# Two up projections with the weights stationary, the first one's operand normed per token tile, modulation product in rows of 1024

## The chip, the core and the metric

The kernel runs on one core of a Trainium2 chip. TensorE (PE in the views) multiplies, VectorE (DVE) and ScalarE (ACT) do element-wise work, GpSimd (POOL) small odds and ends, and SyncE (SP) issues nearly all loads. The metric is device time in microseconds of one execution, the median of several.

## The reference, cut to what matters

Two transformer blocks on 256 tokens of width 2048, in float32, one after the other. Each ends in a feed-forward part with a causal convolution over three tokens:

```python
def conv_ffn(h, w_up, conv_w, conv_b, w_down):      # w_up 2048 x 11264, w_down 5632 x 2048
    up = h @ w_up
    up_p = jnp.pad(up, ((0, 0), (CONV_WIDTH - 1, 0), (0, 0)))
    c = conv_b + sum(conv_w[j] * up_p[:, j:j + S] for j in range(CONV_WIDTH))
    gate, val = jnp.split(c, 2, axis=-1)
    return (jax.nn.silu(gate) * val) @ w_down
...
x = x + conv_ffn(rmsnorm(x, ffn_norm_g), w_up, conv_w, conv_b, w_down)     # first block
...
mod = (silu(c) @ w_mod + b_mod)                     # second block: 2048 -> 6 * 2048, one row
h = rmsnorm_2(x, ffn_pre_w) * (1 + sc_f) + sh_f
x = x + g_f * rmsnorm_2(conv_ffn_2(h, w_up, ffn_conv_w, w_down), ffn_post_w)
```

In front of the feed-forward parts stand the input projections, attention and pooling of the first block, the gated linear attention and short convolution of the second, and an output projection (`w_out`, 2048 x 2048) in each.

## The kernel before, in words

**Products.** Each float32 operand is split in two parts, `hi` (rounded to float32r) and `lo` (what is left); a product is hi*hi + lo*hi + hi*lo. `stream` (line 178 on) runs one pass: it takes 512 (or fewer) columns of a weight matrix, 128 rows at a time (a block `kb`), in loads of four blocks (1 MB, tile `raw`, three buffers). ACT copies two blocks to `hi` (L224), DVE subtracts to `lo` (L225), both with three buffers and placed some way ahead of their turn (`AHEAD`). The activations stand as the stationary operand, 128 features by 128 tokens, the weights move, 512 columns. With two token tiles that is six matmuls per block (L189 hi, L190 lo, L191 the activations' own lo part), 96 in a pass over 2048 rows; the output has tokens on the partitions. `lead` and `trail` put off the second token tile's matmuls at the start or end of a pass, so that the first tile's operand can be used, or the first tile's sums can be worked on, while the second catches up.

**The up passes.** `feed_forward` (L619 on) runs 22 passes over `w_up` (11 pairs of gate and value), each 512 columns wide: ACT copies the two sums to `ev` (L630 or L632), TensorE transposes them to features on the partitions (L270, eight transposes of 128 x 128 into four `aux` banks), ACT and DVE convolve from there (L640 or L643, two at L645 per 128 features), and of the value part DVE and ACT make the `act` operand (L650 to L652) for the down passes. Then four passes over `w_down`, 44 blocks each.

**Between w_out and the first up pass.** `add_residual` (L593) adds each 512-column chunk to `X`, ACT takes the sums of squares, and `operand_chunk` transposes the chunk (eight transposes, L270 `aux<-ident,X`) and splits it, chunk by chunk while the next chunk's pass runs. The norm's factor per token is applied later, when ACT copies the up sums (L632, `scale`).

**Background.** The product silu(c) @ w_mod is cut in 96 jobs, a list that `stream` draws from: each group of four blocks adds a rate (`MOD_IN`, `MOD_UP`, ...) to a counter, and a full counter takes one job. A job loads 1 MB of `w_mod` (tile `rawm`, out of the same three `raw` buffers) and adds four rows of 512 to `macc` on DVE (L306); every fourth job four transposes (L319) and a sum turn `macc` by features.

**Order.** A scheduler places the instructions on each engine; what stands in the program earlier has the better rank, `high_priority` moves it up. PSUM has eight banks: four for `mm`, four for `aux`. All tiles called `big`, `op`, `act`, `gc`, `hl` share sixteen buffers.

## Time and profile before

| | |
|---|---|
| median of 3 runs | 2304.84 us (2304.08 to 2308.02) |
| the profiled execution, its own time | 2303.8 us |
| its span | 2302.0 us |
| TensorE busy | 2264.5 us, 98% |
| VectorE busy | 1575.2 us, 68% |
| ScalarE busy | 1162.9 us, 51% |
| GpSimd busy | 28.6 us, 1% |
| read from memory | 512 MB, 224 GB/s |

Read first which engine is busy nearly all the time, then the chain of work that ended last, then the stretches by stage, and in a stretch how far apart the starts of two instructions of that engine stand: a matmul's own duration in these views includes filling and draining and overlaps the next one's, so that costs are read from starts, not from durations.

### The profile page before, as it was taken

How to read it: one execution, taken by the hardware profiler on the slowest of the kernel's cores; microseconds unless marked ns; L12 is line 12 of the kernel's file. 1: busy time of each engine (PE TensorE's matmuls, PEld its weight loads, DVE VectorE, ACT ScalarE, POOL GpSimd, SP SyncE). 2: the span in 40 equal slices, each digit the busy share in tenths (PEclk: the TensorE clock that was granted, in tenths of full speed). 3: DMA queues.
4: the chain of work that ended last, by engine and by line, in shares of the span. 5: the costliest groups of instructions: out<-in, count | busy, mean ns of one | idle time of the engine just before them, and what ended most of it. 6: DMA issues, size and time to landing. Idle time of an engine off the chain costs nothing.

```text
span 2302.0 us, 27211 instructions
## 1 busy us (share of the span) xinstructions
PE 2264.5 (98%) x10541; PEld 1875.0 (81%) x10541; DVE 1575.2 (68%) x2093; ACT 1162.9 (51%) x1584; POOL 28.6 (1%) x46
## 2 busy tenths in 40 slices
PE   8999999999999999999999999999999999999998
PEld 8878888888888888888797888878888888888886
DVE  5775676778787878666656777776667676674444
ACT  5464554555555555444546444465555555554443
POOL 1001000000000000000000000000000000000000
PEclk9999999999999999999999999999999999999999
DMA  6657456677777777777567656764665666566554
GB/s 227 221 207 255 164 197 227 219 256 252 259 254 257 246 262 264 270 274 257 192 224 242 207 180 240 265 220 165 219 221 200 222 219 223 198 223 213 194 190 146
DMA packets 262391, 516.33 MB, mean 224 GB/s; under 512 B 8567, under 2 KB 21733, under 8 KB 261749
## 3 DMA queue, kind: packets, MB, share of 16 engines
q1 hardware_dynamic: 260256, 510.44, 64.3%
q0 software_dynamic: 1168, 3.77, 0.5%
q8 instruction: 82, 1.34, 0.2%
q10 hardware_dynamic: 837, 0.37, 0.1%
q14 instruction: 48, 0.39, 0.0%
HBM read 512.44 MB, written 2.11 MB: 224 GB/s over the span
## 4 chain that ended last, share of the span: by engine, by line
PE 83%; DVE 6%; DMA 5%; issue 4%; ACT 2%; POOL 0%; SPq 0%; DVEq 0%; POOLq 0%; ACTq 0%
PE mm L190 26%; PE mm L191 26%; PE mm L189 26%; DMA rawm<-in_w_mod 3%; PE aux L270 3%; DVE lo L225 2%; DVE macc L306 1%; ACT hi L224 1%; DMA raw<-in_w_in 1%; PE aux L831 1%; DMA raw<-in_w_down 0%; PE aux L319 0%; DMA raw<-in_w_up 0%; PE aux L578 0%; PE aux L568 0%
## 5 line engine op out<-in xcount | busy, mean ns | idle before, releaser
L225 DVE TENSOR_TENSOR lo<-raw,hi 128x1024 fp32r<-128x1024 f32 (+3 forms) x763 | 914.7, 1202 | 562.3 <-ACT hi L224 560.3
L224 ACT ACTIVATE hi<-raw 128x1024 fp32r<-128x1024 f32 (+3 forms) x763 | 794.3, 1044 | 950.5 <-PE mm L191 768.8
L189 PE MATMUL mm<-hi,op 128*128 128x512 f32 (+3 forms) x2380 | 923.4, 388 | 4.6 <-ACT op L723 2.1
L190 PE MATMUL mm<-lo,op 128*128 128x512 f32 (+3 forms) x2380 | 921.7, 387 | 6.1 <-DVE lo L225 6.1
L191 PE MATMUL mm<-hi,op 128*128 128x512 f32 (+3 forms) x2380 | 919.5, 386 | 0.2 <-DVE op L724 0.2
L189 PEld LDWEIGHTS mm<-hi,op 128*128 128x128 f32 x2380 | 447.8, 188 | 92.4 <-ACT op L723 3.2
L190 PEld LDWEIGHTS mm<-lo,op 128*128 128x128 f32 x2380 | 447.9, 188 | 91.5 <-DVE lo L225 9.3
L191 PEld LDWEIGHTS mm<-hi,op 128*128 128x128 f32 x2380 | 447.7, 188 | 85.6 <-DVE op L724 2.0
L306 DVE SCALAR_TENSOR_TENSOR macc<-rawm,cact,macc 128x512 f32<-128x512 f32 x360 | 269.4, 748 | 43.6 <-DMA rawm<-in_w_mod 37.6
L190 PE MATMUL mm<-lo,act 128*128 128x512 f32 x672 | 262.1, 390 | 0.3 <-DVE lo L225 0.3
L189 PE MATMUL mm<-hi,act 128*128 128x512 f32 x672 | 262.1, 390 | 0.0
L191 PE MATMUL mm<-hi,act 128*128 128x512 f32 x672 | 261.8, 390 | 0.0
L645 DVE SCALAR_TENSOR_TENSOR gc<-aux,cw,gc 128x255 f32<-128x255 f32 (+1 forms) x352 | 147.8, 474 | 7.1 <-ACT gc L643 6.5
L190 PEld LDWEIGHTS mm<-lo,act 128*128 128x128 f32 x672 | 126.2, 188 | 27.6 <-DVE lo L225 1.4
L189 PEld LDWEIGHTS mm<-hi,act 128*128 128x128 f32 x672 | 126.2, 188 | 26.2
L191 PEld LDWEIGHTS mm<-hi,act 128*128 128x128 f32 x672 | 126.2, 188 | 25.9
L270 PE MATMUL aux<-ident,ev 128*128 128x128 f32 x352 | 55.3, 280 | 0.3
L270 PEld LDWEIGHTS aux<-ident,ev 128*128 128x128 f32 x352 | 37.1, 140 | 19.2 <-ACT ev L630 9.9
L640 ACT ACTIVATE gc<-aux,cb,cw 128x256 f32<-128x256 f32 x88 | 42.6, 564 | 3.4 <-PE aux L270 3.4
L651 ACT ACTIVATE act<-gc 128x512 fp32r<-128x512 f32 x44 | 27.7, 629 | 26.0 <-DVE gc L650 26.0
L630 ACT ACTIVATE ev<-mm 128x512 f32<-128x512 f32 x44 | 26.1, 594 | 27.1 <-PE mm L191 26.0
L632 ACT ACTIVATE ev<-mm,rs 128x512 f32<-128x512 f32 x44 | 30.0, 686 | 19.4 <-PE mm L191 19.4
(214 smaller groups left out, 993.3 us busy)
## 6 DMA issues: line engine op xcount, KB each, us to landing
raw<-in_w_up SPq DMA_DIRECT2D x176, 1024.0 KB, 4.9
rawm<-in_w_mod SPq DMA_DIRECT2D x96, 1024.0 KB, 5.4
raw<-in_w_down SPq DMA_DIRECT2D x88, 1024.0 KB, 5.1
raw<-in_w_in SPq DMA_DIRECT2D x72, 1024.0 KB, 5.2
raw<-in_w_out SPq DMA_DIRECT2D x32, 1024.0 KB, 6.1
raw<-in_w_in SPq DMA_DIRECT2D x12, 736.0 KB, 4.8
raw<-in_w_in SPq DMA_DIRECT2D x8, 704.0 KB, 5.4
raw<-in_w_in SPq DMA_DIRECT2D x4, 672.0 KB, 4.1
```

Source lines behind the costliest of these rows:

```text
L189: nc.tensor.matmul(ps[t][:, :n], a[:, tt], hi, start=st, stop=False)
L190: nc.tensor.matmul(ps[t][:, :n], a[:, tt], lo, start=False, stop=False)
L191: nc.tensor.matmul(ps[t][:, :n], b[:, tt], hi, start=False, stop=sp)
L224: nc.scalar.activation(hi[:, :, :n], r, AF.Copy)
L225: nc.vector.tensor_sub(lo[:, :, :n], r, hf[:, :, :n])
L270: nc.tensor.transpose(ps[:width, t * P:(t + 1) * P], src_of_t(t), ident)
L306: nc.vector.scalar_tensor_tensor(acc, raw[:, b], cact[:, k:k + 1], acc, op0=ALU.mult, op1=ALU.add)
L630: nc.scalar.activation(ev[t], ps, AF.Copy)
L632: nc.scalar.activation(ev[t], ps, AF.Identity, scale=evac_scale[:, t:t + 1])
L640: nc.scalar.activation(cv, ps[:, :S], AF.Identity, bias=cb[:, fb:fb + 1], scale=cw[2][:, fb:fb + 1])
L645: nc.vector.scalar_tensor_tensor(cv[:, back:], ps[:, :S - back], cw[2 - back][:, fb:fb + 1], cv[:, back:], op0=ALU.mult, op1=ALU.add)
L651: nc.scalar.activation(act[j][:, two, 0, :], gc[:, 1, two], AF.Copy)
```

## The change

- All up passes but the first of each feed-forward part go through a new function, `stream_up`. The weight tile is the stationary operand, 128 rows by 128 features, and the activations move: `hi` of the weights against both parts of the activations side by side (512 columns: 256 tokens of hi, 256 of lo), then `lo` of the weights against the hi part (256 columns), into the first half of the same bank. The output has features on the partitions, in four banks, which are taken by turns from `aux` and from `mm`. To finish, ACT copies the second half of a bank, DVE adds the first, and the convolution reads the sum from there: there are no transposes and no `ev` copies of 512.
- The first up pass of each part stays as it was, with `lead=16`.
- The operand of the first feed-forward part is made by `Modulated`, which the second one uses already: per token tile, after all four chunks, norm (`finish`), then transposes, scale and split (`split`). The last pass over `w_out` has `trail=14`, and no background jobs.
- The background product takes rows of 1024: 12 pieces of eight jobs in place of 24 of four, each job two rows of 1024 for four of 512, and eight transposes at the end of a piece. The rates are moved a little.
- Some small tiles move into `scr`.

```diff
-MOD_IN, MOD_OUT, MOD_UP, MOD_DOWN = 0.22, 0.35, 0.4, 0.45
+MOD_IN, MOD_OUT, MOD_UP, MOD_DOWN = 0.24, 0.35, 0.36, 0.47
...
+    def stream_up(W, n0, tiles, evac, every):
+        flip[0] ^= 1
+        if flip[0]:
+            ps = [aux([P, 512]) for _ in range(4)]
+        else:
+            ps = [psm.tile([P, 512], F32, tag="mm", name=nm("mm")) for _ in range(4)]
+        for i0 in range(0, 16, 4):
+            raw = wp.tile([P, 4, 512], F32, tag="raw", name=nm("raw"))
...
+            for h in range(0, 4, 2):
+                hi, lo = split_pair(raw, h, 512)
+                for j in range(2):
+                    kb = i0 + h + j
+                    x = tiles[kb // 4][:, kb % 4]
+                    for f in range(4):
+                        fs = slice(f * P, (f + 1) * P)
+                        nc.tensor.matmul(ps[f], hi[:, j, fs], x.rearrange("p a b -> p (a b)"),
+                                         start=kb == 0, stop=False)
+                        nc.tensor.matmul(ps[f][:, :S], lo[:, j, fs], x[:, 0, :], start=False, stop=kb == 15)
...
+        for f in range(4):
+            evac(f, ps[f])
...
-                    holder["acc"] = sm.tile([P, 512], F32, tag="macc", name=nm("macc"), bufs=1)
+                    holder["acc"] = sm.tile([P, 1024], F32, tag="macc", name=nm("macc"), bufs=1)
...
-                for b in range(4):
-                    k = 4 * i + b
+                for b in range(2):
+                    k = 2 * i + b
...
-        operand_chunk(c, xt, g)
+            if c == 3:
+                mod1.finish(t)
...
+            stream(w_out, 512 * c, 512, K16, of(yt), add_residual(c), every=MOD_OUT if c < 3 else 0,
+                   trail=14 if c == 3 else 0)
+    xt = mod1.tiles
...
+                elif stationary:
+                    def up_evac(f, ps, part=part, col=col, gc=gc, j=j):
+                        u = small([P, 512], "ev", 3)[:, :S]
+                        nc.scalar.activation(u, ps[:, S:], AF.Copy)
+                        nc.vector.tensor_tensor(u, ps[:, :S], u, op=ALU.add)
+                        convolve(j, part, f, col // P + f, gc, act[j], u)
+
+                    stream_up(W, col, xt, up_evac, every if j else 0)
...
-    feed_forward(xt, A["w_up"], cw, cb, rs, A["w_down"], first_down, MOD_UP, MOD_DOWN)
+    feed_forward(xt, A["w_up"], cw, cb, None, A["w_down"], first_down, MOD_UP, MOD_DOWN, True)
```

TensorE between two up passes of the first part, before (`mm` are the sums, `ev` the copies that are transposed into `aux`):

```order
L191 MATMUL mm_722_3872<-hi_742_3999,op_486_2580 128x512
L189 MATMUL mm_751_4050<-hi_754_4054,op_483_2577 128x512
L270 MATMUL aux_745_4023<-ident_76,ev_719_3869 128x128
L270 MATMUL aux_746_4029<-ident_76,ev_719_3869 128x128
L270 MATMUL aux_747_4035<-ident_76,ev_719_3869 128x128
L270 MATMUL aux_748_4041<-ident_76,ev_719_3869 128x128
L190 MATMUL mm_751_4050<-lo_755_4055,op_483_2577 128x512
```

TensorE at such a place in the change, where a background piece ends (L280 and L282 are the two matmuls of `stream_up`, L361 the background's transposes):

```order
L280 MATMUL aux_675_3715<-op_554_3005,hi_698_3882 128x512
L282 MATMUL aux_675_3715<-op_554_3005,lo_699_3883 128x256
L280 MATMUL aux_676_3716<-op_554_3005,hi_698_3882 128x512
L282 MATMUL aux_676_3716<-op_554_3005,lo_699_3883 128x256
L361 MATMUL aux_693_3847<-ident_76,macc_418_2213 128x128 x4
L361 MATMUL aux_694_3853<-ident_76,macc_418_2213 128x128 x4
L280 MATMUL mm_706_3934<-op_551_3002,hi_711_3940 128x512
L282 MATMUL mm_706_3934<-op_551_3002,lo_712_3941 128x256
```

The eight transposes of the sums are gone from between the passes. The background's transposes stand between an `aux` pass and an `mm` pass here, and write two of the four `aux` banks that the pass before has just filled.

TensorE from the last pass over `w_out` into the first up pass, before (`ident_76,X_75` are the transposes of a chunk of `X`):

```order
L191 MATMUL mm_551_2953<-hi_573_3087,op_441_2347 128x512
L189 MATMUL mm_600_3163<-hi_603_3167,op_483_2577 128x512
L190 MATMUL mm_600_3163<-lo_604_3168,op_483_2577 128x512
L270 MATMUL aux_577_3109<-ident_76,X_75 128x128
L270 MATMUL aux_578_3114<-ident_76,X_75 128x128
L270 MATMUL aux_579_3119<-ident_76,X_75 128x128
L270 MATMUL aux_580_3124<-ident_76,X_75 128x128
L191 MATMUL mm_600_3163<-hi_603_3167,op_483_2577 128x512
```

The same place in the change (L668 are the transposes of the normed operand, tile `xs`; `hl` are the put-off weights):

```order
L191 MATMUL mm_532_2858<-hl_545_2937,op_440_2332 128x512
L668 MATMUL aux_555_3006<-ident_76,xs_550_2955 128x128 x4
L668 MATMUL aux_557_3018<-ident_76,xs_550_2955 128x128 x4
L668 MATMUL aux_559_3030<-ident_76,xs_550_2955 128x128 x4
L668 MATMUL aux_561_3042<-ident_76,xs_550_2955 128x128 x4
L785 MATMUL aux_569_3070<-ident_76,vstage_568_3068 128x88
L785 MATMUL aux_572_3076<-ident_76,vstage_571_3074 128x88
L189 MATMUL mm_584_3096<-hi_587_3100,op_551_3002 128x512
```

Before, four groups of eight transposes of `X` stood among the matmuls of four passes; now sixteen stand ahead of the first up matmul, and sixteen more some 19 matmuls later.

VectorE behind the end of a value pass of the first part, before (L645 is the convolution, L650 and L652 make `act`, L225 is the weights' `lo`; `aux` are the transposed sums):

```order
L225 TENSOR_TENSOR lo_918_5009<-raw_916_5006,hi_917_5008 128x1024
L645 SCALAR_TENSOR_TENSOR gc_842_4594<-aux_901_4936,cw1_589_3145,gc_842_4594 128x255
L645 SCALAR_TENSOR_TENSOR gc_842_4594<-aux_902_4942,cw1_589_3145,gc_842_4594 128x255
L645 SCALAR_TENSOR_TENSOR gc_842_4594<-aux_901_4936,cw0_586_3139,gc_842_4594 128x254
L645 SCALAR_TENSOR_TENSOR gc_842_4594<-aux_902_4942,cw0_586_3139,gc_842_4594 128x254
L645 SCALAR_TENSOR_TENSOR gc_842_4594<-aux_903_4951,cw1_589_3145,gc_842_4594 128x255
L650 TENSOR_TENSOR gc_842_4594<-gc_842_4594 128x512
L225 TENSOR_TENSOR lo_920_5025<-raw_916_5006,hi_919_5024 128x1024
```

The same place in the change (L752 adds the two halves of a bank, L721 is the convolution, L256 the weights' `lo`, L346 the background; `aux` are the sums of the pass that has ended):

```order
L256 TENSOR_TENSOR lo_776_4375<-raw_772_4352,hi_775_4374 128x1024
L752 TENSOR_TENSOR ev_762_4316<-aux_737_4140,ev_762_4316 128x256
L752 TENSOR_TENSOR ev_763_4322<-aux_738_4141,ev_763_4322 128x256
L752 TENSOR_TENSOR ev_764_4331<-aux_739_4142,ev_764_4331 128x256
L346 SCALAR_TENSOR_TENSOR macc_715_3980<-rawm_782_4436,cact_90,macc_715_3980 128x1024
L721 SCALAR_TENSOR_TENSOR gc_705_3933<-ev_762_4316,cw1_573_3078,gc_705_3933 128x255
L721 SCALAR_TENSOR_TENSOR gc_705_3933<-ev_763_4322,cw1_573_3078,gc_705_3933 128x255
L721 SCALAR_TENSOR_TENSOR gc_705_3933<-ev_762_4316,cw0_570_3072,gc_705_3933 128x254
L721 SCALAR_TENSOR_TENSOR gc_705_3933<-ev_763_4322,cw0_570_3072,gc_705_3933 128x254
L256 TENSOR_TENSOR lo_779_4397<-raw_777_4394,hi_778_4396 128x1024
L725 TENSOR_TENSOR gc_705_3933<-gc_705_3933 128x512
L721 SCALAR_TENSOR_TENSOR gc_705_3933<-ev_764_4331,cw1_573_3078,gc_705_3933 128x255
```

Before, three `lo` of the new pass stood ahead of the sums' work, and six instructions between the third and the fourth; now two stand ahead, and between the second and the third there are three additions, a background row of 1024 and four steps of the convolution.

## Rows read from the trace of the kernel before

**Rows 1.** The page: busy time by engine; chain that ended last; one group.

```profile
PE 2264.5 (98%) x10541; PEld 1875.0 (81%) x10541; DVE 1575.2 (68%) x2093; ACT 1162.9 (51%) x1584; POOL 28.6 (1%) x46
...
PE 83%; DVE 6%; DMA 5%; issue 4%; ACT 2%; POOL 0%; SPq 0%; DVEq 0%; POOLq 0%; ACTq 0%
...
L190 PEld LDWEIGHTS mm<-lo,op 128*128 128x128 f32 x2380 | 447.9, 188 | 91.5 <-DVE lo L225 9.3
```

**Rows 2.** Stretches: up passes 2 to 22 (both parts); an operand made by Modulated.

```profile
core 0: us, PE busy (x) PEld busy (x) DVE busy (x) ACT busy (x) POOL busy (x), PEclk, DMA share, GB/s
402.70:886.71 484.01, 483.11 (x2217) 396.14 (x2216) 384.13 (x521) 266.75 (x327) 0.00 (x0) 1.00 0.72 252
1130.28:1161.66 31.38, 28.35 (x129) 22.38 (x128) 20.94 (x36) 20.27 (x36) 2.92 (x6) 0.95 0.44 152
1570.71:2051.41 480.70, 480.43 (x2195) 393.97 (x2194) 332.32 (x437) 255.46 (x325) 0.00 (x0) 1.00 0.62 210
```

**Rows 3.** Timeline of PE: start, duration, instruction; three boundaries of up passes.

```profile
655.69 0.66 PE L270 MATMUL aux<-ident,ev 128*128 128x128 f32 x4
...
678.49 0.66 PE L270 MATMUL aux<-ident,ev 128*128 128x128 f32 x4
...
701.77 0.66 PE L270 MATMUL aux<-ident,ev 128*128 128x128 f32 x4
```

**Rows 4.** Timeline of PE: two widths, first and last of a run.

```profile
900.22 0.39 PE L190 MATMUL mm<-lo,act 128*128 128x512 f32 x1
...
909.28 0.39 PE L191 MATMUL mm<-hi,act 128*128 128x512 f32 x1
...
1188.64 0.32 PE L190 MATMUL mm<-lo,op 128*128 128x336 f32 x1
...
1198.00 0.32 PE L191 MATMUL mm<-hi,op 128*128 128x336 f32 x1
```

**Rows 5.** Timeline of PE: operand transposes of either kind, and what followed.

```profile
357.05 0.66 PE L270 MATMUL aux<-ident,X 128*128 128x128 f32 x4 [1.07 <-DVE X L593]
...
1130.28 1.91 PE L714 MATMUL aux<-ident,xs 128*128 128x128 f32 x16
1134.02 0.50 PE L189 MATMUL mm<-hi,op 128*128 128x512 f32 x1 [1.83 <-ACT op L723]
```

**Rows 6.** Groups by line and form, count, busy us, mean ns, idle before.

```profile
L225 DVE TENSOR_TENSOR lo<-raw,hi 128x1024 fp32r<-128x1024 f32 x153 | 186.3, 1221 | 69.8 <-ACT hi L224 69.3
...
L306 DVE SCALAR_TENSOR_TENSOR macc<-rawm,cact,macc 128x512 f32<-128x512 f32 x113 | 84.6, 749 | 10.3 <-DMA rawm<-in_w_mod 8.4
...
L645 DVE SCALAR_TENSOR_TENSOR gc<-aux,cw,gc 128x255 f32<-128x255 f32 x76 | 34.0, 474 | 0.0
...
L652 DVE TENSOR_TENSOR act<-gc,act 128x512 fp32r<-128x512 f32 x20 | 13.7, 684 | 0.2 <-ACT act L651 0.2
...
L640 ACT ACTIVATE gc<-aux,cb,cw 128x256 f32<-128x256 f32 x76 | 36.7, 564 | 2.5 <-PE aux L270 2.5
```

**Rows 7.** The same view of the whole span: 256 columns on DVE and ACT.

```profile
L865 DVE TENSOR_TENSOR E<-E,qk 128x256 f32<-128x256 f32 x14 | 5.8, 415 | 0.0
...
L630 ACT ACTIVATE ev<-mm 128x512 f32<-128x512 f32 x44 | 26.1, 594 | 27.1 <-PE mm L191 26.0
...
L570 ACT ACTIVATE big<-aux 128x256 f32<-128x256 f32 x8 | 2.9, 383 | 2.8 <-PE aux L568 2.8
```

**Rows 8.** Timeline of DVE in the first up passes: how closely instructions follow.

```profile
566.29 2.04 DVE L645 SCALAR_TENSOR_TENSOR gc<-aux,cw,gc 128x255 f32<-128x255 f32 x5
...
570.68 1.22 DVE L225 TENSOR_TENSOR lo<-raw,hi 128x1024 fp32r<-128x1024 f32 x1
...
572.41 1.22 DVE L225 TENSOR_TENSOR lo<-raw,hi 128x1024 fp32r<-128x1024 f32 x1
573.55 0.68 DVE L652 TENSOR_TENSOR act<-gc,act 128x512 fp32r<-128x512 f32 x1
...
603.64 3.11 DVE L306 SCALAR_TENSOR_TENSOR macc<-rawm,cact,macc 128x512 f32<-128x512 f32 x4
```

More of the change, by code (lines that the diff above doesn't have):

```diff
@@ L345, in body @@
     for i in (0, 1, 3, 2, 4, 5):
-        for c in range(4):
-            background.extend(mod_piece(4 * i + c, by_feature(i)))
+        for c in range(2):
+            background.extend(mod_piece(2 * i + c, by_feature(i)))
     ss = small([P, NT, 4], "ss")
@@ L602, in body @@
-    head, tail = list(range(8)), list(range(8, 16))
-    open_ps = []
-    for c in range(2):
-        open_ps.append(stream(w_out, 512 * c, 512, head, of(yt), None, last=False, every=MOD_OUT))
-        mix(c)
-    xt = pair_tiles(16)
-    for c in range(4):
-        if c < 2:
-            stream(w_out, 512 * c, 512, tail, of(yt), add_residual(c), ps=open_ps[c], first=False, every=MOD_OUT)
-        else:
-            stream(w_out, 512 * c, 512, K16, of(yt), add_residual(c), every=MOD_OUT)
-        operand_chunk(c, xt, g)
@@ L659, in conv_columns @@
-    def conv_columns(ap3, name):
-        tiles = []
-        for j in range(3):
-            tiles.append(wide_columns(ap3[j], f"{name}{j}"))
-        return tiles
-    def wide_columns(ap1, name):
-        stage = small([P, P], "vstage", 2)
-        nc.scalar.dma_start(stage[:88, :], ap1.rearrange("(r p) -> r p", p=P))
-        ps = aux([P, 512])
-        nc.tensor.transpose(ps[:, :88], stage[:88, :], ident[:88, :88])
-        dst = cst.tile([P, 88], F32, tag="wide_" + name[-1], name=nm(name))
-        nc.vector.tensor_copy(dst, ps[:, :88])
-        return dst
@@ L726, in body, with add_residual, go @@
     late = {}
+    mod1 = Modulated(vec("ffn_norm_g"))
+    def add_residual(c):
+        def go(t, ps):
+            cs = slice(c * 512, (c + 1) * 512)
+            nc.vector.tensor_tensor(X[:, t, cs], ps, X[:, t, cs], op=ALU.add)
+            mod1.chunk(t, c)
+            if c == 3:
+                mod1.finish(t)
+        return go
+    head, tail = list(range(8)), list(range(8, 16))
+    open_ps = []
+    for c in range(2):
+        open_ps.append(stream(w_out, 512 * c, 512, head, of(yt), None, last=False, every=MOD_OUT))
+        mix(c)
@@ new lines, in conv_columns, with wide_columns @@
+    def conv_columns(ap3, name):
+        tiles = []
+        for j in range(3):
+            tiles.append(wide_columns(ap3[j], f"{name}{j}"))
+        return tiles
+    def wide_columns(ap1, name):
+        stage = small([P, P], "vstage", 2)
+        nc.scalar.dma_start(stage[:88, :], ap1.rearrange("(r p) -> r p", p=P))
+        ps = aux([P, 512])
+        nc.tensor.transpose(ps[:, :88], stage[:88, :], ident[:88, :88])
+        dst = cst.tile([P, 88], F32, tag="wide_" + name[-1], name=nm(name))
+        nc.vector.tensor_copy(dst, ps[:, :88])
+        return dst
@@ L728, in first_down @@
+    cw = conv_columns(A["conv_w"], "cw")
+    cb = wide_columns(A["conv_b"], "cb")
     def first_down(c):
```

179 lines of the change are left out of this document (101 added, 78 removed).

## The prediction

> **What bounds the kernel now.** I read the page's busy times and chain first: TensorE is busy 98% of the span and 83% of the chain that ended last is its own work [rows 1]. Other engines matter only where TensorE waits for them. Then the stretches that the change touches. The 21 up passes from the second on take 484.01 us in the first part and 480.70 us in the second, with TensorE busy for all but a microsecond and its granted clock at 1.00, the upper level, 2.4 GHz, [rows 2]. So an up pass costs what TensorE has to do in it, and I price that from the starts of its instructions.
>
> Two such prices. From L190 at 900.22 to L191 at 909.28 are 40 matmuls of 512 columns: 226.5 ns each. From 1188.64 to 1198.00 are 61 of 336 columns: 153.4 ns each [rows 4]. The 176 columns between cost 73.1 ns, 0.4154 ns a column, and some 13.8 ns are left that do not depend on the width. A pass of 96 matmuls of 512 is 21.74 us. Passes begin 22.80 us apart (the transposes at 655.69 and 678.49), or 23.28 with four background transposes (678.49 to 701.77) [rows 3]. The eight transposes of the sums thus cost 1.06 us a pass, four of the background 0.48 us, and none of it is hidden.
>
> **The change, part by part.** The sum is made against the profiled execution's 2303.8 us; the median is 1.0 us above that.
>
> *Up passes.* Per block the six matmuls of 512 columns become four of 512 and four of 256: as many columns, two matmuls more. No row shows float32r on 256 columns. On the line of the two widths one costs 153.4 - 80 x 0.4154 = 120.2 ns. Bounds: below, 109 ns, the spacing of transposes, each of which loads its own 128 columns of weights for 128 columns of work ((1.91 - 0.27) us over 15) [rows 5]; above, the 153.4 ns of 336 columns. I take 120, since two widths lie on the line and only a limit of the load could bend it. A pass is then 64 x (226.5 + 120.2) ns = 22.19 us. Before: 964.71 us for 42 passes less 44 background transposes (by the counts: 2217 - 2016 - 168 = 33, and 11) at 0.48 us per four, 5.3 us, is 959.4 us. After: 42 x 22.19 = 932.0 us. **-27.4 us.** Transposes of the two passes that stay as they were are paid as before, those of the two last passes fall away, so the stretches' edges cancel.
>
> A rule of the Trainium skill gives another price: TensorE: Matmul & The Clock Gate, section Back-to-back issue gap, has a warm matmul cost its columns over 2.4 GHz plus 2.5 ns. By that the 1344 additional matmuls would cost 3.4 us in place of 18.5, and the time would be some 15 us lower; the rows of 512 and 336 columns show 13.8 ns, and I go by them.
>
> *Background.* 24 groups of four transposes become 12 of eight; four more in a row cost 4 x 109 ns: 12 x 0.92 - 24 x 0.48 = **-0.5 us**. Loads are as many and as large. On DVE the work shrinks (below).
>
> *Operand of the first part.* Before: four groups of eight transposes among passes that run on, 1.06 us each, and one wait of 1.07 us at 357.05 [rows 5]: 5.3 us. After, it is made as the second block's first operand is made, by the same function: from the first transposes at 1130.28 to the end of the next pass 31.38 us, 9.6 above a plain pass, with 1.83 us of waiting in one place and a mean clock of 0.95 in the stretch [rows 2, 5]. The put-off matmuls (`trail=14`, 42 of them, 9.5 us) cover the norm of the first token tile; what is late is the split of the first four blocks. **+4.3 us**; 0 if `trail=14` and `lead=16` cover more than the eight there, 9 if the clock falls for longer.
>
> *Banks after the first pass of part one.* The eight transposes fill all four `aux` banks, and the first `stream_up` pass wants the same four. TensorE waits for the copy of the second token tile (0.59, rows 7), then per bank for ACT's 0.56 and two steps of DVE; steps follow each other at (2.04 - 0.47)/4 = 0.39 us, eight of them take 3.1 us [rows 6, 8]. Of that about 5 us one matmul round (1.4 us) and the transposes run beside it: **+3 us**, between 0 and 5. Before, this was hidden, since the next pass had its own banks. In part two the first `stream_up` pass takes `mm` banks, and this does not arise.
>
> *Background transposes behind an `aux` pass.* Twice in part one they write banks whose sums were just finished: ACT's copy (0.38) and DVE's addition (0.42) come first [rows 7]. The first bank's last matmul is three pairs, 1.04 us, older than the pass's end: about 0.5 us each, **+1 us**, at most 2.5.
>
> *VectorE in part one.* Additions are new, 4 x about 0.34 a pass; background rows get cheaper: 4 x 0.787 ((3.11 - 0.75)/3) = 3.15 us a job becomes 2 x 1.32 (0.787 plus the 0.538 by which 1024 columns exceed 512, 1221 - 683 ns) = 2.65 us [rows 6, 8]. A pass has 8 x 1.14 (`lo`) + 8 x 0.39 + 1.36 + 1.2 (products, `act`) + 1.44 jobs x 2.65 = 18.6 us, of 22.2: 84%. Before it was 18.5 of 22.9. There is room on average, but behind a value pass three additions, a row of 1024 and four steps stand ahead of the third `lo`, and with what follows the fourth `lo` ends, counted from the pass's end, at 0.6 + 1.3 + 1.6 + 1.1 + 0.6 + 0.4 + 0.3 + 0.6 + 0.4 + 1.1 = 8.0 us, when TensorE wants it at 3 x 2.77 = 8.3 us. It is close: **+2 us** for part one, from 0 up to the second rival. Part two has half the jobs: nothing.
>
> Sum: -27.4 - 0.5 + 4.3 + 3 + 1 + 2 = -17.6, so 2286.2 us for the profiled execution and **2287 us** for the median.
>
> **The rivals.** *The weights' load shows (slower).* Before, each load had a matmul of 512 columns to hide behind; now every second one has 256, 107 ns of streaming. If the next load can begin only when the `lo` matmul begins, that matmul lasts as long as load and change-over. The spacing of transposes puts a load at 109 ns; with the 13.8 ns that is 123 ns, 2688 x 3 ns = 8 us, still faster (2295 us). It decides from 120.2 + 17.6 us/2688 = 126.7 ns; at the bound of 153.4 it is +89 us, 2376 us; halfway between, 137 ns, 2332 us. For it: no row has float32r under 336 columns. Against it: loads recorded as 188 ns [rows 1] follow each other at 153 ns without leaving the line [rows 4]. The Trainium skill (same page, section LDWEIGHTS) puts a load at its columns over 1.2 GHz, 107 ns for 128, which is a tie with the streaming and speaks against this change; the transposes' 109 ns agree.
>
> *VectorE becomes the bound in part one (no change).* If the tight place behind a pass's end costs 0.8 us in each of 21 passes, 17 us go back: 2304 us. For it: 84% busy, in order, with ACT's results to wait for (69.8 us of idle time ahead of `lo`, nearly all for ACT [rows 6]). Against it: before the change DVE had stretches as long without `lo` (566.29 to 570.68 [rows 8]), and TensorE was idle for under a microsecond of that part's 484 [rows 2].
>
> *The fixed part is smaller (faster).* If the `lo` matmul costs no more than the load's 109 ns, 2688 x 11 = 30 us more are gained: 2257 us.
>
> **How the numbers follow.** Forecast 0.70 (its own range 2275 to 2299: the bounds of the operand, bank and DVE terms, and 115 to 123 ns for the `lo` matmul); load shows beyond its point 0.10; DVE bound 0.13; smaller fixed part 0.07. The range from 2270 to 2307 adds the DVE rival and leaves out the load rival and most of the last. A measurement of this kernel can tell about 0.2%, 4.6 us, from no change. Faster by more: 0.70 + 0.07 + 0.02 of the DVE rival = 0.79; within: 0.10, nearly all DVE; slower: 0.10 from the load and 0.01 from DVE.
>
> **What would show it.** In the profile after: pairs of matmuls 346.7 ns apart in the up passes, the `lo` one's start 226.5 behind the `hi` one's and the next 120 later; 22.2 us from pass to pass, in both parts alike; no L270-like transposes of `ev` but in two passes; a wait of some 3 us at the start of part one's second pass for the `aux` banks; under 2 us of TensorE's idle time charged to `lo` in part one. The prediction is wrong if the pair takes more than 353 ns, if part one's passes come out over 23 us while part two's do not, or if the stretch from the last pass over w_out to the second up pass loses more than 15 us.

## The result, and the profile after

The changed kernel takes 2281.28 us (median of 4 runs, 2277.82 to 2282.99), the kernel before beside it 2304.46 us: a ratio of 0.9891, 95% interval 0.9875 to 0.9907, 23.2 us less where 17.6 were forecast. Its profiled execution took 2280.28 us, with a span of 2278.5 us. The rows that answer to [rows 1], from the page of the changed kernel, with the two matmuls of `stream_up` (L280 the one of 512 columns, L282 the one of 256) and the background's row:

```profile
PE 2248.5 (99%) x11549; PEld 1912.1 (84%) x11549; DVE 1601.4 (70%) x2071; ACT 1181.1 (52%) x1680; POOL 30.7 (1%) x47
...
PE 94%; DVE 2%; DMA 2%; ACT 1%; issue 1%; POOL 0%; SPq 0%; DVEq 0%; POOLq 0%; ACTq 0%
...
L280 PE MATMUL aux<-op,hi 128*128 128x512 f32 x1344 | 472.6, 397 | 1.8 <-ACT gc L717 1.8
...
L282 PE MATMUL mm<-op,lo 128*128 128x256 f32 x1344 | 375.5, 280 | 0.2 <-DVE lo L256 0.2
...
L346 DVE SCALAR_TENSOR_TENSOR macc<-rawm,cact,macc 128x1024 f32<-128x1024 f32 x180 | 230.5, 1281 | 22.7 <-DMA rawm<-in_w_mod 20.9
```

TensorE's share of the chain went from 83% to 94%, VectorE's from 6% to 2%, the loads' from 5% to 2%. So two things happened: TensorE's own work became less, and it waits less for others. The stretches (the last pass over w_out with the first up pass, up passes 2 to 22 of part one, the four down passes, the passes over w_out_2, up passes 2 to 22 of part two), columns as in [rows 2]:

```profile
348.89:402.33 53.44, 49.99 (x238) 40.49 (x236) 33.75 (x59) 32.15 (x57) 1.12 (x2) 1.00 0.50 178
402.33:879.17 476.84, 476.59 (x2720) 413.93 (x2721) 391.39 (x525) 266.48 (x362) 0.00 (x0) 1.00 0.70 247
879.17:1124.08 244.91, 243.07 (x1091) 201.48 (x1089) 161.43 (x161) 105.66 (x120) 0.54 (x1) 1.00 0.73 262
1432.60:1526.43 93.83, 92.61 (x428) 76.46 (x426) 72.56 (x92) 47.98 (x71) 2.04 (x2) 1.00 0.76 270
1555.94:2028.78 472.84, 472.82 (x2703) 411.78 (x2702) 355.01 (x488) 264.08 (x367) 0.00 (x0) 1.00 0.62 215
```

The two up stretches went from 484.01 and 480.70 [rows 2] to 476.84 and 472.84 us: 15.0 us, about half of the 27.4 forecast for them. The rest came from where the forecast had next to nothing: the passes over w_in are 3.9 us shorter, the first down passes 2.4, the passes over w_in_2 5.6.

**The pair of matmuls has two spacings.** TensorE's timeline at the start of two passes, columns as in [rows 3]:

```profile
493.79 0.40 PE L280 MATMUL aux<-op,hi 128*128 128x512 f32 x1
494.04 0.28 PE L282 MATMUL aux<-op,lo 128*128 128x256 f32 x1
494.15 0.40 PE L280 MATMUL aux<-op,hi 128*128 128x512 f32 x1
...
516.41 0.40 PE L280 MATMUL mm<-op,hi 128*128 128x512 f32 x1
...
653.33 0.40 PE L280 MATMUL mm<-op,hi 128*128 128x512 f32 x1
653.56 0.28 PE L282 MATMUL mm<-op,lo 128*128 128x256 f32 x1
653.68 0.39 PE L280 MATMUL mm<-op,hi 128*128 128x512 f32 x1
...
675.51 0.40 PE L280 MATMUL aux<-op,hi 128*128 128x512 f32 x1
```

From 493.79 to 516.41 are 64 pairs in 22.62 us (most passes of this kind take 22.61, 353.3 ns a pair); from 653.33 to 675.51 they take 22.18 us (22.187 unrounded, 346.7 ns a pair). I call the first spacing wide, the second narrow. The narrow sum is the forecast's 226.5 + 120.2 to the tenth; its halves are not. On average the short matmul starts 232 ns behind the long one and the next long one 115 ns behind that; in the wide pass it is 237 and 117 ns. Between the two spacings there is little: the passes of the trace keep one of the two for many passes and then change (at 617 to 625, 759, 1769, 1839 and 1904 us). 214 of the 336 groups of eight pairs stand at the wide spacing, some 27 of 42 passes, which costs 214 x 8 x 6.67 ns = 11.4 us against narrow spacing throughout. 27.4 less 11.4 is 16.0. The stretches are 15.0 us shorter, since the background's transposes (5.3 us before, 4.6 after) and 1.7 us of other delays stand in them too.

### The profile page after: what moved, and what is told of

It reads as the page before. It is cut to its first block, busy times and chain, and to the rows that moved or that the text cites. A ratio compares the mean times of both kernels' runs of the same rounds, so it can differ in the third digit from the quotient of the medians.

```text
span 2278.5 us, 29454 instructions
## 1 busy us (share of the span) xinstructions
PE 2248.5 (99%) x11549; PEld 1912.1 (84%) x11549; DVE 1601.4 (70%) x2071; ACT 1181.1 (52%) x1680; POOL 30.7 (1%) x47
## 4 chain that ended last, share of the span: by engine, by line
PE 94%; DVE 2%; DMA 2%; ACT 1%; issue 1%; POOL 0%; SPq 0%; DVEq 0%; POOLq 0%; ACTq 0%
PE mm L190 17%; PE mm L189 17%; PE mm L191 17%; PE aux L280 13%; PE mm L280 13%; PE aux L282 7%; PE mm L282 7%; DMA rawm<-in_w_mod 1%; PE aux L310 1%; DMA raw<-in_w_in 1%; PE aux L896 1%; PE aux L361 0%; DVE lo L225 0%; PE aux L910 0%; PE aux L621 0%
## 5 line engine op out<-in xcount | busy, mean ns | idle before, releaser
L225 DVE TENSOR_TENSOR lo<-raw,hi 128x1024 fp32r<-128x1024 f32 (+3 forms) x415 | 490.8, 1186 | 350.1 <-ACT hi L224 349.4
L224 ACT ACTIVATE hi<-raw 128x1024 fp32r<-128x1024 f32 (+3 forms) x415 | 426.9, 1031 | 560.0 <-PE mm L191 496.3
L256 DVE TENSOR_TENSOR lo<-raw,hi 128x1024 fp32r<-128x1024 f32 x336 | 409.3, 1221 | 192.3 <-ACT hi L255 191.4
L280 PE MATMUL aux<-op,hi 128*128 128x512 f32 x1344 | 472.6, 397 | 1.8 <-ACT gc L717 1.8
L280 PE MATMUL mm<-op,hi 128*128 128x512 f32 x1344 | 472.9, 397 | 0.0
L189 PE MATMUL mm<-hi,op 128*128 128x512 f32 (+3 forms) x988 | 378.9, 383 | 4.4 <-ACT op L303 2.3
L190 PE MATMUL mm<-lo,op 128*128 128x512 f32 (+3 forms) x988 | 375.7, 380 | 1.4 <-DVE lo L225 1.4
L191 PE MATMUL mm<-hi,op 128*128 128x512 f32 (+3 forms) x988 | 375.6, 380 | 0.5 <-DVE op L683 0.5
L282 PE MATMUL aux<-op,lo 128*128 128x256 f32 x1344 | 375.6, 280 | 0.1
L282 PE MATMUL mm<-op,lo 128*128 128x256 f32 x1344 | 375.5, 280 | 0.2 <-DVE lo L256 0.2
L280 PEld LDWEIGHTS aux<-op,hi 128*128 128x128 f32 x1344 | 252.1, 188 | 62.8 <-ACT gc L717 2.0
L280 PEld LDWEIGHTS mm<-op,hi 128*128 128x128 f32 x1344 | 252.2, 188 | 60.5
L282 PEld LDWEIGHTS aux<-op,lo 128*128 128x128 f32 x1344 | 253.4, 189 | 0.7 <-DVE lo L256 0.5
L282 PEld LDWEIGHTS mm<-op,lo 128*128 128x128 f32 x1344 | 253.2, 189 | 0.8 <-DVE lo L256 0.7
L346 DVE SCALAR_TENSOR_TENSOR macc<-rawm,cact,macc 128x1024 f32<-128x1024 f32 x180 | 230.5, 1281 | 22.7 <-DMA rawm<-in_w_mod 20.9
L189 PEld LDWEIGHTS mm<-hi,op 128*128 128x128 f32 x988 | 186.6, 189 | 38.6 <-ACT op L682 3.2
L191 PEld LDWEIGHTS mm<-hi,op 128*128 128x128 f32 x988 | 186.6, 189 | 33.4 <-DVE op L683 2.7
```

Source lines behind the costliest of these rows:

```text
L189: nc.tensor.matmul(ps[t][:, :n], a[:, tt], hi, start=st, stop=False)
L190: nc.tensor.matmul(ps[t][:, :n], a[:, tt], lo, start=False, stop=False)
L191: nc.tensor.matmul(ps[t][:, :n], b[:, tt], hi, start=False, stop=sp)
L224: nc.scalar.activation(hi[:, :, :n], r, AF.Copy)
L225: nc.vector.tensor_sub(lo[:, :, :n], r, hf[:, :, :n])
L256: nc.vector.tensor_sub(lo[:, :, :n], r, hi.bitcast(F32)[:, :, :n])
```

## The experiments

**Rows of 512 again.** The changed kernel with the old background product:

```diff
-                raw = wp.tile([P, 2, 1024], F32, tag="raw", name=nm("rawm"))
+                raw = wp.tile([P, 4, 512], F32, tag="raw", name=nm("rawm"))
...
-                for b in range(2):
+                for b in range(4):
```

> The changed kernel with the background product in rows of 512 again (24 groups of four jobs, four rows of 512 a job, four transposes a group); all else as changed. Theory A: the time gained outside the up passes (3.6 us in the passes over w_in, 2.5 in the first down passes, 5.6 in the passes over w_in_2) comes from the wider rows, which leave VectorE more room; then this kernel gives back some 12 us and the half microsecond of transposes, and runs in 2293 us, with the same pair spacings in the up passes. Rival B: those gains come from the background's jobs falling at other moments; then it gives back 2 us at most, 2281 to 2284 us.

2300.88 us, 0.9981 (0.997 to 0.9992) of the kernel before. So the wider rows are worth more in the changed kernel than even A said: some four fifths of its gain go with them. The stretches that answer to the third and fourth above:

```profile
883.72:1136.20 252.48, 246.41 (x1091) 200.70 (x1089) 169.01 (x196) 104.07 (x120) 0.54 (x1) 1.00 0.73 255
1449.55:1547.57 98.02, 94.87 (x429) 77.28 (x427) 74.99 (x105) 48.03 (x71) 2.10 (x2) 0.98 0.73 258
```

The down passes take 7.6 us more and the passes over w_out_2 4.2 us more, where the up form is the same; the passes over w_in_2 between them take 4.8 us more. VectorE has only 7.6 and 2.4 us more to do in the two stretches shown and is far from full; what is lost stands at single places (in the down passes 23 delays with 6.4 us together, in the changed kernel 0.2 us), the first of them just behind the up passes:

```profile
891.90 0.39 PE L189 MATMUL mm<-hi,act 128*128 128x512 f32 x1
893.64 0.50 PE L190 MATMUL mm<-lo,act 128*128 128x512 f32 x1 [1.35 <-DVE lo L225]
```

The two up stretches take 950.1 us here, as many as in the changed kernel, but not because nothing is lost there. Only 111 of the 336 groups were wide in this trace, which costs 5.9 us; transposes and delays make up 12.2 us of the 950.1, against 6.3 in the changed kernel. How many groups are wide differs from execution to execution, as a later run shows, and is worth up to 17.9 us, so it is also a part of what separates the medians in this section.

**Rows of 1024 alone.** The kernel before with that part of the change (rates and small tiles with it):

```diff
-                raw = wp.tile([P, 4, 512], F32, tag="raw", name=nm("rawm"))
+                raw = wp.tile([P, 2, 1024], F32, tag="raw", name=nm("rawm"))
```

> The kernel before with the background product in rows of 1024 (12 groups of eight jobs, the new rates, the small tiles in scr) and nothing else of the change. Theory A: the wider rows relieve VectorE wherever it runs close to TensorE, in either form of the up passes, so most of the 20 us that they were worth in the changed kernel show here too: the 12 us of the passes over w_in, the first down passes and the passes over w_in_2 at least, 2294 us or less. Theory B: they are worth 20 us only together with the stationary up passes, whose additions fill VectorE up; with the old up passes they give no more than the prediction's half microsecond of transposes and the small waits, 2302 to 2306 us.

2294.83 us beside 2305.71 us of the kernel before: 10.9 us less, 0.9945 (0.993 to 0.9961). A, though not all of the 20 us: the rest shows only together with the stationary form. Its profiled execution was the slowest of five and shows 5 us of the gain (2.7 in the passes over w_in); where the other 6 lie isn't shown.

**Everything but the stationary form.** The call of the second part gets the same `False`.

```diff
-    feed_forward(xt, A["w_up"], cw, cb, None, A["w_down"], first_down, MOD_UP, MOD_DOWN, True)
+    feed_forward(xt, A["w_up"], cw, cb, None, A["w_down"], first_down, MOD_UP, MOD_DOWN, False)
...
-                    stream(W, col, 512, K16, of(xt), evac, every=every)
+                    stream(W, col, 512, K16, of(xt), evac, every=every if j else 0,
+                           lead=0 if j or part else 16)
```

> The changed kernel with all up passes in the old form (activations stationary, eight transposes of the sums), both parts; the first part's operand normed per token tile and the rows of 1024 stay. By the prediction's working the up passes cost 959.4 us in the old form; in the changed kernel's trace they cost 932 us and 11.4 us of slow pairs, with a wait of 2 us for banks: this kernel should be 14 us above the changed one, 2295 us, if the stationary form brings what the pairs show, and 4 us above the kernel before with rows of 1024 alone, if the operand costs what the prediction said. If VectorE takes part of the stationary form's gain back, it is less than 14 us above the changed kernel.

2294.79 us, 0.9948 (0.9933 to 0.9963): 13.5 us above the changed kernel, as expected, and level with the rows of 1024 alone. The stretches that answer to the first, second and last above:

```profile
350.13:401.68 51.55, 50.37 (x233) 41.25 (x232) 32.65 (x55) 29.76 (x53) 1.12 (x2) 0.97 0.56 190
401.68:884.78 483.10, 482.81 (x2215) 396.24 (x2214) 365.85 (x448) 262.31 (x325) 0.00 (x0) 1.00 0.72 244
1562.48:2042.57 480.09, 479.82 (x2191) 393.63 (x2189) 326.94 (x406) 255.08 (x325) 0.00 (x0) 1.00 0.63 211
```

The up stretches, 963.19 us here and 949.68 in the changed kernel, differ by the same 13.5 us. The first stretch is 1.9 us longer in the changed kernel: the wait for the `aux` banks. In the run with rows alone it took 47.94 us, and the three passes ahead 2.0 us more than here: moving the operand costs 3.6 - 2.0 = 1.6 us by the traces and nothing by the medians.

**No background.** What sets the spacing? First the changed kernel without the product.

```diff
-        for c in range(2):
-            background.extend(mod_piece(2 * i + c, by_feature(i)))
+        pass
...
         nc.vector.tensor_copy(bmod, ps[:, :96])
+        nc.vector.tensor_copy(mod, bmod)
```

> The changed kernel without the background product: silu(c) @ w_mod is left out (its 96 loads, VectorE's rows and sums, TensorE's transposes), the modulation is the bias alone. In the changed kernel a pair of matmuls (512 and 256 columns) in an up pass takes either 346.7 or 353.3 ns, and stays with one of them over several passes. Theory P: which of the two is set where the row of matmuls was last broken, by a split part that comes late or by transposes, and then lasts; without background nothing breaks it, so each part keeps the spacing of its first stationary pass (353.3 in the changed kernel), 22.61 us a pass from the third to the last. Rival C: 353.3 is what other work on the memory (VectorE's rows, loads) costs; without background all pairs take 346.7 ns, 22.19 us a pass. Either way the time falls by the 11 us of transposes and by waits outside the up passes: about 2262 us by P, 2252 us by C.

The trace (2257.62 us) has the pairs of both parts at 346.7 ns, but for the first few. So the spacing stays where nothing comes between, as P has it, but not at the one that I took for given. The other three runs took 2267.56 to 2268.38 us; one part at the wide spacing would account for 21 x 0.43 = 9 of these 10 us, but they have no trace.

**Breaks without load.** The same, with eight transposes of a constant behind every fourth up pass:

```diff
                     stream_up(W, col, xt, up_evac, every if j else 0)
+                    if j and (2 * j + part) % 4 == (0 if cb is not None else 3):
+                        for _ in range(2):
+                            ps = aux([P, 512])
+                            for q in range(4):
+                                nc.tensor.transpose(ps[:, q * P:(q + 1) * P], ident, ident)
```

> The changed kernel without the background product (silu(c) @ w_mod is left out, the modulation is the bias alone), and with eight transposes of a constant on TensorE behind every fourth stationary up pass; no work for VectorE, no loads come with them. Without them all pairs of matmuls took 346.7 ns in the trace. Theory P (the spacing is set anew where the row of matmuls is broken, and lasts until the next break): the spacing changes, if it does, only at these places, and of the ten to twelve stretches between them some run at 353.3 ns, 22.61 us a pass. Rival C (353.3 ns is what VectorE's rows and the loads cost): all stretches run at 346.7 ns, 22.19 us a pass, and only the transposes' 0.92 us are added behind every fourth.

One pass of part one and one of part two:

```profile
450.16:472.78 22.62, 22.62 (x131) 19.60 (x130) 14.47 (x21) 12.86 (x18) 0.00 (x0) 1.00 0.58 186
1579.08:1601.26 22.18, 22.18 (x130) 19.56 (x129) 16.62 (x26) 12.71 (x19) 0.00 (x0) 1.00 0.60 190
```

All of part one ran wide, all of part two narrow; none of the ten groups of transposes changed it. Both theories lose something. C falls: wide spacing without any of VectorE's rows or the background's loads. And a break by transposes between passes is not enough, against P. What holds in these two runs is that a part enters with one of the two and keeps it.

**The changed kernel once more, as it is.**

> The changed kernel as it is, profiled once more. Theory P (which of the two spacings a part starts with, and where it changes, is decided anew in each execution): other passes run at 353.3 ns than in the first profile (28 of 42, beginning slow in both parts). Rival F (the program's order fixes it): the same passes, with changes at the same places.

2279.55 us, with 180 groups of 336 wide. Part one began wide, part two narrow, where it had begun wide in the first profile. In part two the spacing changed at the same three places in both, in opposite directions. The first of them, in the first profile (passes of 22.61 us before it, 22.19 behind it) and in this one (22.19, then 22.61):

```profile
1768.34 0.40 PE L280 MATMUL aux<-op,hi 128*128 128x512 f32 x1
1768.57 0.28 PE L282 MATMUL aux<-op,lo 128*128 128x256 f32 x1
1768.69 0.40 PE L280 MATMUL aux<-op,hi 128*128 128x512 f32 x1
```

```profile
1764.94 0.39 PE L280 MATMUL aux<-op,hi 128*128 128x512 f32 x1
1765.17 0.28 PE L282 MATMUL aux<-op,lo 128*128 128x256 f32 x1
1765.29 0.39 PE L280 MATMUL aux<-op,hi 128*128 128x512 f32 x1
1765.54 0.39 PE L282 MATMUL aux<-op,lo 128*128 128x256 f32 x1
```

The next `lo` was finished 0.26 and 0.06 us ahead of its first matmul here, and so at the third place; at the second stand the background's transposes, in the middle of a pass. In part one the places differ: the first profile has two changes there, this one eight, and of these ten nine stand at a `lo` that was finished less than 0.4 us ahead of its first matmul (the tenth at the background's transposes). Four others as late changed nothing in the first profile. So in the changed kernel a close `lo` or a row of transposes is where the spacing can change, not what it changes to. F falls.

**lo one block behind.** If a late `lo` changes the spacing, wanting it later should leave fewer changes:

```diff
-                        nc.tensor.matmul(ps[f][:, :S], lo[:, j, fs], x[:, 0, :], start=False, stop=kb == 15)
+                        if behind:
+                            lw, lx = behind
+                            nc.tensor.matmul(ps[f][:, :S], lw[:, fs], lx, start=False, stop=False)
+                    behind = lo[:, j], x[:, 0, :]
...
+        lw, lx = behind
+        for f in range(4):
+            nc.tensor.matmul(ps[f][:, :S], lw[:, f * P:(f + 1) * P], lx, start=False, stop=True)
```

So the first four long matmuls of a pass and its last four short ones stand in a row.

> The changed kernel with the matmuls of 256 columns one block behind: hi of a block by turns with lo of the block before, so that lo is wanted 1.4 us later and the alternation stays. Theory P: with lo never late the spacing of the pairs changes at the background's transposes and the starts of the parts alone, is 346.7 or 353.3 ns in between, and which it is decides between 2270 and 2288 us; the waits for lo go, about 2 us in part one. Rival L (353.3 ns comes from lo's lateness itself): all pairs at 346.7 ns, 2268 to 2270 us.

2290.55 us, 0.9929 (0.9914 to 0.9944), slower than the change and beyond P's 2288. In part two, where every `lo` was ready at least 2.2 us ahead of its matmul, all 21 passes ran wide. L falls: wide pairs with no late `lo`. In part one, where four were still less than 0.4 us ahead, the spacing changed seven times, five of them between two passes. Some 34 wide passes instead of 27 are 3 us of the 9; the last up pass took 24.9 us (22.2 in the changed kernel) and the down pass behind it 62.4 (60.8), another 4.

**Other orders in a block.** Four long and four short, eight and eight, and long, short, short, long:

```diff
-                    for f in range(4):
-                        fs = slice(f * P, (f + 1) * P)
-                        nc.tensor.matmul(ps[f], hi[:, j, fs], x.rearrange("p a b -> p (a b)"),
-                                         start=kb == 0, stop=False)
-                        nc.tensor.matmul(ps[f][:, :S], lo[:, j, fs], x[:, 0, :], start=False, stop=kb == 15)
+                    for f in range(4):
+                        nc.tensor.matmul(ps[f], hi[:, j, f * P:(f + 1) * P], x.rearrange("p a b -> p (a b)"),
+                                         start=kb == 0, stop=False)
+                    for f in range(4):
+                        nc.tensor.matmul(ps[f][:, :S], lo[:, j, f * P:(f + 1) * P], x[:, 0, :],
+                                         start=False, stop=kb == 15)
```

> The changed kernel with another order in a block: the four matmuls of 512 columns first, then the four of 256, in place of one of each by turns. Theory N: a matmul costs its columns and a fixed part, whatever stands beside it, and the 353.3 ns come only from the alternation: 4 x (226.5 + 120.2) = 1387 ns a block, 22.19 us a pass, and the time falls by the 11.4 us of slow pairs to 2270 us. Rival L: the load of the weights is what the 353.3 ns show, and behind a matmul of 256 columns a load of 256's matmul cannot hide: four matmuls of 256 in a row take 126.7 ns or more each, 1413 ns a block or more, 22.61 us a pass in all 42 passes, and the time rises to 2288 us or above.

Eight and eight:

```diff
+                for j in range(2):
+                    ...
+                        nc.tensor.matmul(ps[f], hi[:, j, f * P:(f + 1) * P], x.rearrange("p a b -> p (a b)"),
+                                         start=kb == 0, stop=False)
+                for j in range(2):
+                    ...
+                        nc.tensor.matmul(ps[f][:, :S], lo[:, j, f * P:(f + 1) * P], x[:, 0, :],
+                                         start=False, stop=kb == 15)
```

> As the run before, over two blocks: eight matmuls of 512 columns, then eight of 256, so that the lo part is wanted 1.6 us later than in the changed kernel. Theory N: 2 x 1387 ns for two blocks, 2270 us, and no matmul waits for lo. Rival L: 2 x 1413 ns or more, 2288 us or above. If the lateness of lo costs something by itself, this run is faster than the one before; if not, they are equal within 1 us.

Long, short, short, long:

```diff
+                        ...
+                        for go in (short, long) if f % 2 and 0 < kb < 15 else (long, short):
+                            go()
```

> The changed kernel with another order in a block: long, short, short, long (512, 256, 256, 512 columns) in place of long and short by turns, except in the first and the last block of a pass. By runs of four and of eight a pair took 350.8 and 349.2 ns, with one spacing throughout. Theory N (each switch between widths and each run adds a fixed part): runs of two lie between, one spacing of 346.7 to 351 ns, 22.2 to 22.45 us a pass, and the time is 2276 to 2288 us. If it comes out at 346.7 ns it beats the changed kernel by some 11 us, 2270 us. Rival P: two spacings as in the changed kernel, 2281 us.

| order | undisturbed pass | a pair | time | ratio to before |
|---|---|---|---|---|
| by turns (the change) | 22.19 or 22.61 us | 346.7 or 353.3 ns | 2281.28 us | 0.9891 (0.9875 to 0.9907) |
| four and four | 22.45 us | 350.8 ns | 2286.28 us | 0.9917 (0.9904 to 0.9931) |
| eight and eight | 22.35 us | 349.2 ns | 2281.02 us | 0.9892 (0.9879 to 0.9906) |
| long, short, short, long | 22.34 us | 349.1 ns | 2281.64 us | 0.9881 (0.986 to 0.9902) |

Each other order has one spacing, the same in every undisturbed pass, between the two. For the first two of them neither N's 346.7 nor L's 353.3 came; for the last N's range held (346.7 to 351 ns, 2276 to 2288 us), and P's two spacings did not come. None beats the change by more than the intervals. Eight and eight is 5.3 us faster than four and four; 4.3 of that are its pairs, so that the later `lo` brings no more than 1 us, which the noise hides.

The runs of four also show which of the two matmuls is dearer than the forecast's 226.5 and 120.2 ns:

```profile
700.01 1.09 PE L279 MATMUL aux<-op,hi 128*128 128x512 f32 x4
700.94 0.64 PE L282 MATMUL aux<-op,lo 128*128 128x256 f32 x4
701.42 1.09 PE L279 MATMUL mm<-op,hi 128*128 128x512 f32 x4
```

By the starts four long ones take 0.93 us, 232 ns each, and four short ones 0.48 us (118.6 ns each, unrounded over 12 us). With eight and eight it is 230 and 119 ns. In these orders it is the long one; why it is dearer here than in the down passes is open.

**The short matmul's size.** 128 columns in place of 256, and 320:

```diff
-nc.tensor.matmul(ps[f][:, :S], lo[:, j, fs], x[:, 0, :], start=False, stop=kb == 15)
+nc.tensor.matmul(ps[f][:, :P], lo[:, j, fs], x[:, 0, :P], start=False, stop=kb == 15)
```

> The changed kernel with the lo part of the weights multiplied by 128 columns in place of 256; the lo product of the second token tile is left out. Theory T (tie: the load of 128 columns of weights, 109 ns by the spacing of transposes, is as long as the streaming of 256 columns, and is what holds the short matmul up): the pair stays at 346 ns or falls by a few ns, and the time stays within 15 us of the changed kernel's 2281 us. Rival D (columns decide, the load is hidden): the short matmul falls by 128 x 0.4154 = 53 ns to 67 ns, the pair to 293 ns, and the time by some 140 us, to 2140 us, if ScalarE and VectorE keep up.

```diff
+nc.tensor.matmul(ps[f][:, :320], lo[:, j, fs], x.rearrange("p a b -> p (a b)")[:, :320],
+                 start=False, stop=kb == 15)
```

> The changed kernel with the lo part of the weights multiplied by 320 columns in place of 256 (the 256 of hi and the first 64 of lo, a product that the kernel leaves out otherwise). By the line of widths the short matmul takes 146.7 ns, the pair 373.3 ns, a pass 23.89 us. Theory T (the two spacings of the pair come from the tie of load and streaming): with 64 columns more the load is hidden with room, and all pairs in both parts have one spacing, 373 ns; 2281 - 11.4 + 71.6 = 2341 us. Rival D (the two spacings have another origin): again two, 373 and 380 ns, 23.89 and 24.32 us a pass, with stretches of either.

TensorE with 128 columns, then with 320:

```profile
700.13 0.22 PE L282 MATMUL mm<-op,lo 128*128 128x128 f32 x1
700.19 0.44 PE L280 MATMUL mm<-op,hi 128*128 128x512 f32 x1
700.47 0.22 PE L282 MATMUL mm<-op,lo 128*128 128x128 f32 x1
700.53 0.44 PE L280 MATMUL mm<-op,hi 128*128 128x512 f32 x1
```

```profile
700.01 0.40 PE L280 MATMUL aux<-op,hi 128*128 128x512 f32 x1
700.24 0.31 PE L282 MATMUL aux<-op,lo 128*128 128x320 f32 x1
700.39 0.40 PE L280 MATMUL aux<-op,hi 128*128 128x512 f32 x1
```

With 128 columns the undisturbed pair takes 340 ns (700.19 to 700.53; passes of 21.76 us): half the columns save 7 to 13 ns, not 53, and D falls. Less the 226.5 of a long matmul that is 113 ns, less the 232 of a long one in a row 108, close to the 109 of a transpose in a row [rows 5]. That it is the load which costs this is T's argument and not shown: the starts alone lie 60 ns behind the short one and 280 ns behind the long one. The Trainium skill (TensorE: Matmul & The Clock Gate, section LDWEIGHTS) puts a load at its columns over 1.2 GHz, an estimate of 107 ns for 128, and the rest of the pair agrees with it. With 320 columns the pair takes 380.0 ns in both parts, 24.32 us a pass, one spacing only, as T says; but not T's 373.3. By the starts the short one takes 146 ns, T's 146.7, and the long one ahead of it 234 in place of 226.5. Two spacings were seen only where a short matmul of 256 columns stands alone between long ones.

The time with 128 columns was 2344.08 us, 63 more, against T's 15. For the most part this is the waits' doing:

```profile
PE mm L282 <- DVE lo L256: 28.3, 23, 4.2
PE aux L282 <- DVE lo L256: 21.6, 20, 2.8
```

In the changed kernel these waits come to 0.2 us together. Another part is the clock, which fell at times. Here the engine had stood idle for 2.00 us before:

```profile
495.50 0.33 PE L282 MATMUL mm<-op,lo 128*128 128x128 f32 x1 [2.00 <-DVE lo L256]
...
497.16 0.74 PE L280 MATMUL mm<-op,hi 128*128 128x512 f32 x1
497.70 0.31 PE L282 MATMUL mm<-op,lo 128*128 128x128 f32 x1
497.80 0.73 PE L280 MATMUL mm<-op,hi 128*128 128x512 f32 x1
```

From 496.2 to 499.5 us the granted clock was 0.50, the lower level, 1.2 GHz, and a pair took 640 ns (497.16 to 497.80). Some 68 pairs of the up passes were as slow, which costs 20 us. The scheduler also gave VectorE another order here (in part one a row of the background stands just ahead of a `lo` 38 times, 26 times in the changed kernel), so this isn't the price of shorter passes alone; 2359.87 us with 320 columns is what its pairs make of it.

## Why the prediction came out

The bound was right, and so was the mechanism in the up passes: TensorE's own work sets their time, and it became less. That 2287 stood so near to 2281 is in part luck, two errors that cancel: the up passes gave 11.4 us less than forecast, the background 10.4 more.

| step | forecast | the runs |
|---|---|---|
| up passes | -27.4 us | -16.0: -27.4 at the narrow spacing, +11.4 for the wide one |
| background: transposes, rows | -0.5 | -10.9, by itself |
| operand of the first part | +4.3 | +1.6 by the traces, 0 by the medians |
| banks after the first pass | +3 | +1.9 |
| transposes behind an `aux` pass, VectorE in part one | +1, +2 | +1.7 together |
| sum | -17.6 | -21.7, measured -23.2 |

The 1.7 us are what the two up stretches (949.68 us) hold beside their pairs (932.0 + 11.4) and five groups of eight transposes (0.92 each). The -10.9 is the worth of the rows without the rest of the change; beside the stationary form it was 19.6 (2300.88 to 2281.28), so the table is one way of adding up, not the only one.

- **Up passes.** The step that failed is the price of a pair as the sum of two numbers, each read from rows of its own width in passes where the weights move. 226.5 + 120.2 ns is right for a third of the pairs; the others take 353.3. The runs of four and of eight put the excess on the long matmul (232 and 230 ns in place of 226.5); the short one took 119, no more than said. The rival "the weights' load shows" put its point at 126.7 ns for the short one, a pair of 353.2, so its price came in two thirds of the pairs, at the very point from which it eats the gain; and by the prediction's own sign (a pair over 353 ns) the forecast of this part was wrong there. Its reason, the load, is not shown, and the short matmuls in a row, each with a load of its own, speak against it. The other sign held: both parts behave alike.
- **Background.** This was the big miss. The prediction had found the cheaper rows (3.15 to 2.65 us a job; the means of 749 and 1281 ns make it 3.0 and 2.56) and used them only in part one's balance of VectorE. But jobs run beside nearly every stage, and one in front of a `lo` delays it. What TensorE waited for (time, times, longest), in the changed kernel with rows of 512:

```profile
PE mm L190 <- DVE lo L225: 5.1, 8, 1.3
...
PE aux L359 <- DVE macc L346: 3.1, 2, 2.7
```

and in the changed one, which has none of the second kind:

```profile
PE mm L190 <- DVE lo L225: 1.4, 2, 1.2
```

The same line for the kernel before and for the rows of 1024 alone:

```profile
PE mm L190 <- DVE lo L225: 6.4, 10, 1.2
```

```profile
PE mm L190 <- DVE lo L225: 5.8, 5, 2.3
```

So beside the stationary form the longer rows shortened such waits. By themselves they hardly did in this trace, that of their slowest run (with the operand moved as well it was 2.1 us); most of their 10.9 us is not explained by these waits, and what brings it stays open. The step left out is: where else does this instruction stand ahead of one that TensorE wants?
- **VectorE as the bound.** With rows of 1024 the rival did not come (0.2 us of waits). With rows of 512 four fifths of the gain were gone, 2300.88 us, close to the rival's 2304, but not in the way that it says: by the traces 16.6 us went in the down passes, the passes over w_in_2 and those over w_out_2, and what the up passes lost to delays, some 5 us more than in the changed kernel, their spacing gave back. The parts are not independent: rows alone 10.9 us, the stationary form and operand alone about 5 (2306.01 to 2300.88), both together 23.2.
- **Operand and banks.** As forecast in kind, smaller in size. The wait stands where it was put, at the second pass of part one:

```profile
399.89 0.66 PE L310 MATMUL aux<-ident,ev 128*128 128x128 f32 x4 [0.25 <-ACT ev L740]
402.33 0.47 PE L280 MATMUL aux<-op,hi 128*128 128x512 f32 x1 [1.78 <-ACT gc L717]
```

- **The fixed part.** The Trainium skill's 2.5 ns (same page, section Back-to-back issue gap), which that section gives for a matmul by itself, without the load that each has here, is not seen: 768 columns over 2.4 GHz are 320 ns, and 26.7 or 33.3 ns are left for the two matmuls of a pair.

Open is what picks the spacing when a part begins, and why some breaks change it and others don't. Shown: it is not the program's order alone (two profiles of one program differ), not the background's load (wide without it, narrow with it), and not a late `lo` (wide where none was within 0.9 us).

## What to carry to other kernels

Price background work not by its sum but by what each of its instructions can stand in front of: fewer, longer rows on an engine that is 70% busy were worth 10.9 us by themselves, the work taken from the engine that is 98% busy 13.5. Where matmuls of two widths are to stand by turns, the sum of their prices from other rows is only an estimate of the pair; measure the pair itself, in other orders and with a smaller and a larger size beside it. And change two such things together only with each of them also measured alone: here the gain of the one depended on the other.

## What the hardware did that I had not expected

- The same pair of matmuls, in the same order, at the same granted clock of 1.00, ran for hundreds of microseconds at 346.7 or at 353.3 ns, and which of them differed between executions of one program.
- Short matmuls in a row, each with its load, aren't dearer than by turns: runs of two, four and eight lie between the two spacings of the change (349.1 to 350.8 ns a pair). In runs of four a matmul of 256 columns took 119 ns, one of 512 took 232, where the down passes of the kernel before show 226.5 for 512.
- With 128 columns in the short matmul in place of 256 a pair still took 340 ns, 7 to 13 less, where the columns alone would save 53.
